# One channel tile of a depthwise convolution as diagonal products on TensorE, with three smaller edits around it

## The chip, the cores and the metric

The kernel runs on one core of one Trainium2 chip (trn2). The metric is device time in microseconds (us). TensorE is called PE in the profile (PEld is its weight load, PEclk its granted clock), VectorE is DVE, ScalarE is ACT, GpSimd is POOL, SyncE is SP. L970 is line 970 of the kernel's file.

## The reference, cut to what matters

A trunk of two layers works on 640 tokens of width 1024: 128 prompt tokens and 512 sample tokens. The change lies in layer 0, where one input projection feeds attention and a convolution module, and both share the output projection.

```python
h = x * (1 + scale) + shift                       # adaLN, vectors from silu(cond) @ w_ada
q, k, v, u = split(h @ w_in)                      # 512, 128, 128, 1024 columns
q, k = rmsnorm(q), rmsnorm(k)                     # per head of 64; rotary for sample tokens
att = softmax(q @ k.T / 8) @ v                    # 8 heads, 2 kv heads; sample sees 512 + 128 cached
a, gt = split(u, 2)
u = a * sigmoid(gt)                               # 512 channels
u = depthwise_conv(u, conv_w, width=31) + conv_b  # per channel, along the tokens of each request
u = silu(layernorm(u, conv_ln_g, conv_ln_b))      # over the 512 channels
x = layernorm(ALPHA * x + gate * (concat(att, u) @ w_out))
```

A squared-ReLU MLP, an mLSTM layer and a second MLP follow; the change leaves them alone.

## The kernel before, in words

Everything lives in SBUF as tiles of 128 partitions. A float32 operand of a large product is split into two fp32r parts, hi and lo, and every such product is three products on PE (`mm3`, L193 to L195). ScalarE makes the hi part of a weight piece (L166), GpSimd the lo part (L167).

The stage that the change touches runs in the profiled execution from about 62 to 325 us.

**Input projection, 62 to 186 us.** `GEMMS = "01k2qr3"` sets the order. A digit is a channel tile of the convolution: `glu(i)` makes two halves of the a and gate products (320 of the 640 tokens each), ScalarE takes tanh of the gate (`sg`, L977), VectorE multiplies into the padded array `up` (L981), and `conv(i)` (L950) follows. `k` is the key and value group, `q` and `r` two groups of query heads: five token tiles of products (128x256), evicted into the tile `acc`, then `chain`, which normalises per head on VectorE. `chain` calls `rsqrt_here` (L389), 15 short VectorE operations with three Newton steps; the conv norm calls it too.

**The convolution.** `up` has 128 channels on partitions and 655 output columns: 128 prompt tokens, 15 columns of padding, 512 sample tokens. A tap k is `cy += cw[k] * up[k:k+655]`. `CONV_DVE` says by channel tile which taps go to VectorE, as one operation each (L965; L956 for k = 0). Any other tap is an ACT product into a tile `tap` of two buffers (L970) and a GpSimd addition (L972). Tiles 0 and 1 have all 31 taps on VectorE, tile 2 every 4th, tile 3 every 8th. The conv has low priority (`CONV_BEHIND`): the framework's scheduler puts its taps behind other ready work, and so fixes the order of each engine's queue.

**Late adaLN vectors.** `background()` issues one k-step of a pending adaLN vector: four narrow PE products (128x32 weights, L293). After eight steps VectorE adds the bias (L297), and PE transposes the result (L305). Such steps stand between the tiles of the projection and between the units of attention. They use the one PSUM tile of `psc`.

**Attention, 186 to 325 us.** Twelve units (i, u): head pair i, u = -1 for the prompt rows, 0 and 1 for the sample rows. `weights_of` of the next unit makes scores (L1187), then `softmax`: VectorE maximum (L1152), ScalarE exp (L1154), VectorE reciprocal (L1155) and VectorE division (L1157). `values_of` transposes the weights on PE (L1219), copies them (L1222, L1224) and multiplies by v (L1226). Behind unit 8 (`NORM_AT`), the input rows are loaded again for the residual, and `conv_norm` runs in one piece: products with a matrix of ones for the mean (L1255, float32) and for the variance (L1269), `rsqrt_here`, diagonal products (L1280), and the swish.

Of the kernel before, what the change touches and what calls it, by code (L numbers as in the profile page):

```python
# [9 lines left out]
F32 = mybir.dt.float32  # L10
# [8 lines left out]
P = 128  # L19
# [39 lines left out]
LATE_DVE = 0  # L59
CONV_DVE = (range(31), range(31), range(0, 31, 4), range(0, 31, 8))  # L60
PT_ACT = (0,)
NORM_AT = 8
CN_DVE = (1, 1)
# [29 lines left out]
def trunk_kernel(ctx: ExitStack, tc: tile.TileContext, I, O):  # L93
# [297 lines left out]
    def rsqrt_here(out, var, n, scale):  # L391

        v, a = (smallp.tile([P, 20], F32, name=f"rh_{x}", bufs=1)[:, 0:n] for x in "va")
        g = out.bitcast(I32)
        nc.vector.tensor_scalar(out=v, in0=var, scalar1=scale, scalar2=EPS, op0=ALU.mult, op1=ALU.add)
        nc.vector.tensor_scalar(out=g, in0=v.bitcast(I32), scalar1=1, scalar2=None, op0=ALU.arith_shift_right)
        nc.vector.tensor_scalar(
            out=g, in0=g, scalar1=-1.0, scalar2=float(0x5F3759DF), op0=ALU.mult, op1=ALU.add)
        for _ in range(3):
            nc.vector.tensor_tensor(out=a, in0=out, in1=out, op=ALU.mult)  # L400
            nc.vector.tensor_tensor(out=a, in0=a, in1=v, op=ALU.mult)
            nc.vector.tensor_scalar(out=a, in0=a, scalar1=-0.5, scalar2=1.5, op0=ALU.mult, op1=ALU.add)
            nc.vector.tensor_tensor(out=out, in0=a, in1=out, op=ALU.mult)

    def rsqrt_one(r, var):
# [510 lines left out]
    with ExitStack() as m0s:  # L916
# [13 lines left out]
        if True:  # L930
            cvp = qcs.enter_context(tc.tile_pool(name="cvp", bufs=1, reuse_waits="tile"))
            cv2 = qcs.enter_context(tc.tile_pool(name="cv2", bufs=2, reuse_waits="tile"))
            qk = qcs.enter_context(tc.tile_pool(name="qk", bufs=1, reuse_waits="tile"))

            up = upp.tile([P, 4, UW], F32, name="up")
# [12 lines left out]
            S0 = PAD + SEQ + PAD  # L948

            def conv(i):  # L950

                y = cy[:, i, :]
                with tc.high_priority(offset=-CONV_BEHIND):
                    dve = CONV_DVE[i]
                    if 0 in dve:
                        nc.vector.tensor_scalar(  # L956
                            out=y, in0=up[:, i, 0:CW], scalar1=cw[:, i, 0:1], scalar2=cols[:, 64 + i:65 + i],
                            op0=ALU.mult, op1=ALU.add)
                    else:
                        nc.scalar.activation(  # L960
                            out=y, in_=up[:, i, 0:CW], func=AF.Identity, scale=cw[:, i, 0:1],
                            bias=cols[:, 64 + i:65 + i])
                    for k in range(1, CONV_K):
                        if k in dve:
                            nc.vector.scalar_tensor_tensor(  # L965
                                out=y, in0=up[:, i, k:k + CW], scalar=cw[:, i, k:k + 1], in1=y,
                                op0=ALU.mult, op1=ALU.add)
                        else:
                            tp = upp.tile([P, CW], F32, name="tap", bufs=2)
                            nc.scalar.activation(  # L970
                                out=tp, in_=up[:, i, k:k + CW], func=AF.Copy, scale=cw[:, i, k:k + 1])
                            nc.gpsimd.tensor_tensor(out=y, in0=y, in1=tp, op=ALU.add)  # L972
# [18 lines left out]
            def glu(i, steps=2):  # L991
                us = u_w[0] if i == 0 else u_units(i)
                for half in range(2):
                    ps = u_ps[half] if i == 0 else ps2()
                    pa, pg = ps[:, 0], ps[:, 1]
                    ks = range(4, 8) if i == 0 else range(KT)
                    fm_half(us[1], half, pg, ks)
                    fm_half(us[0], half, pa, ks)
                    background(steps)
                    gated(i, half, lambda: pa, pg)  # L1000
                conv(i)
# [51 lines left out]
            def chain(x, c0, n):  # L1053
# [10 lines left out]
                rr = smallp.tile([P, NT, n], F32, name=f"rr{n}", bufs=1)  # L1064
                rsqrt_here(
                    rr.rearrange("p t h -> p (t h)"), ss.rearrange("p t h -> p (t h)"), NT * n, 1.0 / HD)
# [21 lines left out]
            def kv_group():  # L1088
                ws = load_n256(w_in, ATT_W)
                put_k(ck, NT)  # L1090
                for t in range(NT):
# [3 lines left out]
                    nc.vector.tensor_copy(out=qkv[:, t, ATT_W:ATT_W + KV_W], in_=ps[:, 0:128])  # L1095
                    background(1)
                nc.sync.dma_start(out=O["new_cache_v"][0, 0], in_=vS[:, 0, :].rearrange("p (g d) -> p g d", d=HD))
                kn = chain(1, ATT_W, KVH)
# [3 lines left out]
            def q_group(grp, kn=None):  # L1102
                ws = load_n256(w_in, grp * 256)
                for t in range(NT):
                    ps = ps1()
                    tm_tile(ws, act, t, ps[:, 0:256])
                    nc.scalar.copy(out=qkv[:, t, grp * 256:(grp + 1) * 256], in_=ps[:, 0:256])
                    background(1)
                    if kn is not None:
                        put_k(kn[:, t], t)  # L1110
                chain(0, grp * 256, 4)

            kn = None
            for what in GEMMS:
                if what == "k":
# [3 lines left out]
                else:  # L1119
                    glu(int(what), 3)  # L1120
            drain()


# [22 lines left out]

        def softmax(ps, dst, multi):

# [7 lines left out]
            d2 = dst.rearrange("p a b -> p (a b)") if multi else dst  # L1156
            nc.vector.tensor_scalar(out=d2, in0=d2, scalar1=ri[:, 0:1], scalar2=None, op0=ALU.mult)  # L1157

# [5 lines left out]
        def weights_of(i, s):  # L1164
# [3 lines left out]
            if s < 0:  # L1168
# [6 lines left out]
                for h in range(2):  # L1175
                    softmax(sp[:, h, 0:P], pp[:, h, :], False)
                Ps[i, s] = pp
                return
            pts = [[], []]
            for t in (1 + 2 * s, 2 + 2 * s):  # L1180
                for h in range(2):
# [7 lines left out]
                    pt = att.tile([P, 2, HT], F32, name="ptok", bufs=PTOK)  # L1189
                    softmax(s2[:, :, 0:HT], pt, True)  # L1190
                    pts[h].append(pt.rearrange("p a b -> p (a b)"))
# [44 lines left out]
        def conv_norm():  # L1236
# [14 lines left out]
            for half in range(2):  # L1251
# [5 lines left out]
                for (c0, n, o) in segs(half):  # L1257
                    y = cy[:, :, c0:c0 + n]
                    nc.vector.tensor_tensor(out=y, in0=y, in1=wide(pm, o, n), op=ALU.subtract)
            sq = []  # L1260
            for i in range(4):
# [10 lines left out]
            rc = smallp.tile([P, NT], F32, name="rc", bufs=1)  # L1272
            rsqrt_here(rc, pv[:, 0:NT], NT, 1.0)
            for ts in ((0, 1, 2, 3), (4,)):
# [6 lines left out]
                for c0, n, o in ((0, P, 0), (PAD + P, 3 * P, P)) if len(ts) > 1 else ((PAD + 4 * P, P, 0),):  # L1281
                    y = cy[:, :, c0:c0 + n]
                    nc.vector.tensor_tensor(out=y, in0=y, in1=wide(pr, o, n), op=ALU.mult)

            for i in range(4):
# [6 lines left out]
                for c0, n, o in ((0, P, 0), (PAD + P, DEC, P)):  # L1292
                    hi, lo = (x[:, 4 + i, o:o + n] for x in act)
                    nc.scalar.copy(out=hi, in_=cy[:, i, c0:c0 + n])
                    CN_LO[i % 2].tensor_tensor(out=lo, in0=cy[:, i, c0:c0 + n], in1=f32(hi), op=ALU.subtract)

        ada_late = [(0, 5)] + [(1, v) for v in range(6)]
# [4 lines left out]
        for n, (i, u) in enumerate(units):  # L1302
# [6 lines left out]
            if n == NORM_AT:  # L1309
# [5 lines left out]
                cl = cls.enter_context(tc.tile_pool(name="cl", bufs=1, side="right", reuse_waits="tile"))  # L1315
                conv_norm()
        cls.close()
# [610 lines left out]
```

## Time and profile before

| | |
|---|---|
| median of three runs | 1735.19 us (1735.14 to 1742.12) |
| profiled execution | 1737.0 us, span 1735.2 us, mean granted clock 0.97 |
| PE busy | 1607.3 us, 93% of the span |
| DVE busy | 1098.1 us, 63% |
| ACT busy | 796.3 us, 46% |
| POOL busy | 1005.4 us, 58% |

The page gives shares over the whole program. The change touches only 62 to 325 us, so the views are asked for that stretch. A window's line gives each engine's busy time in it. A wait's line names the waiting instruction, then the one that it waited for. A group's line counts instructions of one source line and shape, with busy time and mean duration, and behind the last bar the idle time of that engine just before them.

### The profile page before, as it was taken

Reading aid. Unit: us, or ns where it says so; the run is one execution under the profiler, and the core shown is the slowest. Engines: PE = TensorE matmul, PEld = TensorE weight load, DVE = VectorE, ACT = ScalarE, POOL = GpSimd, SP = SyncE. Lnnn points to the kernel's source line nnn. Section 1 sums busy time; section 2 is a strip of 40 time slices with the busy share of each in tenths; the row PEclk is TensorE's granted clock in tenths of the full one; section 3 lists DMA queues with packets and bytes.
Section 4 is the critical chain, followed back from the end, with each engine's and each line's share of the span. In section 5 each row is a group of like instructions: output and inputs, shape, how many; then the busy total and the mean of one; then the engine's idle time right before and its main releaser. Section 6 shows DMA issues by size and latency. Waiting matters only on the chain. (4 is left out here: it accounts for less than half of the span.)

```text
span 1735.2 us, 27401 instructions
## 1 busy us (share of the span) xinstructions
PE 1607.3 (93%) x10155; PEld 1412.7 (81%) x10155; DVE 1098.1 (63%) x1924; ACT 796.3 (46%) x1560; POOL 1005.4 (58%) x760
## 2 busy tenths in 40 slices
PE   7988899998989999999788998997989999999996
PEld 4678555898879989987678998897979889989885
DVE  2899997669434444356875687778498354344367
ACT  2224666345444344343543555556265444344343
POOL 2246474247955546548654766756459756546565
PEclk8999999998999999999999999999999999999998
DMA  9852885323432213216223222235442323213241
GB/s 307 256 185 75 268 306 178 71 101 119 130 85 92 92 56 97 86 61 206 83 69 103 71 84 91 98 98 194 123 152 85 125 89 98 89 57 98 85 158 61
DMA packets 151309, 211.76 MB, mean 122 GB/s; under 512 B 11845, under 2 KB 92969, under 8 KB 151176
## 3 DMA queue, kind: packets, MB, share of 16 engines
q1 hardware_dynamic: 150944, 209.94, 37.4%
q8 instruction: 80, 1.31, 0.3%
q14 instruction: 53, 0.43, 0.1%
q10 hardware_dynamic: 232, 0.08, 0.0%
HBM read 186.74 MB, written 23.24 MB: 121 GB/s over the span
## 5 line engine op out<-in xcount | busy, mean ns | idle before, releaser
L167 POOL TENSOR_TENSOR wlo<-raw,whi 128x512 fp32r<-128x512 f32 x374 | 518.6, 1410 | 412.2 <-ACT whi L166 397.5
L166 ACT CAST whi<-raw 128x512 fp32r<-128x512 f32 x368 | 224.7, 620 | 429.2 <-PE ps L195 192.1
L193 PE MATMUL ps<-whi,h 128*128 128x512 f32 x640 | 254.5, 399 | 11.0 <-DVE pr L526 5.7
L194 PE MATMUL ps<-wlo,h 128*128 128x512 f32 x640 | 254.6, 398 | 0.3 <-POOL wlo L167 0.3
L195 PE MATMUL ps<-whi,h 128*128 128x512 f32 x640 | 253.6, 396 | 0.0
L193 PE MATMUL ps<-act_h,whi 128*128 128x320 f32 (+2 forms) x704 | 221.2, 316 | 8.5 <-ACT act_h L625 7.5
L194 PE MATMUL ps<-act_l,whi 128*128 128x320 f32 (+2 forms) x704 | 221.3, 315 | 5.5 <-DVE act_l L626 3.1
L195 PE MATMUL ps<-act_h,wlo 128*128 128x320 f32 (+2 forms) x704 | 220.9, 314 | 2.2 <-POOL wlo L167 2.2
L167 POOL TENSOR_TENSOR wlo<-s,whi 128x512 fp32r<-128x512 f32 x118 | 163.9, 1393 | 67.2 <-ACT whi L166 61.9
L758 DVE TENSOR_TENSOR acc<-acc,ps 128x512 f32<-128x512 f32 x120 | 81.8, 685 | 162.0 <-PE ps L195 162.0
L193 PEld LDWEIGHTS ps<-whi,h 128*128 128x128 f32 x640 | 121.3, 190 | 40.2 <-DVE pr L526 6.0
L193 PEld LDWEIGHTS ps<-act_h,whi 128*128 128x128 f32 x704 | 135.3, 192 | 13.2 <-ACT act_h L625 7.9
L195 PEld LDWEIGHTS ps<-whi,h 128*128 128x128 f32 x640 | 121.3, 190 | 29.2
L194 PEld LDWEIGHTS ps<-wlo,h 128*128 128x128 f32 x640 | 121.5, 190 | 28.1 <-POOL wlo L167 1.2
L194 PEld LDWEIGHTS ps<-act_l,whi 128*128 128x128 f32 x704 | 134.9, 192 | 8.9 <-DVE act_l L626 3.9
L195 PEld LDWEIGHTS ps<-act_h,wlo 128*128 128x128 f32 x704 | 134.9, 192 | 3.1 <-POOL wlo L167 3.1
L193 PE MATMUL ps<-whi,act_h 128*128 128x256 f32 x440 | 126.1, 290 | 0.3 <-DVE acc L1095 0.3
L194 PE MATMUL ps<-wlo,act_h 128*128 128x256 f32 x440 | 124.7, 287 | 0.0
L195 PE MATMUL ps<-whi,act_l 128*128 128x256 f32 x440 | 123.8, 287 | 0.0
L972 POOL TENSOR_TENSOR cy<-cy,tap 128x655 f32<-128x655 f32 x50 | 80.3, 1606 | 54.0 <-DVE cy L965 22.6
L193 PE MATMUL ps<-T_h,whi 128*128 128x320 f32 x336 | 103.7, 309 | 1.6 <-ACT pr L550 1.6
L166 ACT CAST whi<-s 128x512 fp32r<-128x512 f32 x120 | 73.2, 616 | 67.3 <-DVE s L501 54.9
(437 smaller groups left out, 4066.0 us busy)
## 6 DMA issues: line engine op xcount, KB each, us to landing
raw<-in_w_ff_dram SPq DMA_DIRECT2D x128, 512.0 KB
whi<-in_w_ada_dram SPq DMA_DIRECT2D x80, 256.0 KB
wlo<-in_w_ada_dram SPq DMA_DIRECT2D x80, 256.0 KB
raw<-in_w_in_m_dram SPq DMA_DIRECT2D x32, 512.0 KB
ada_w<-in_w_ada_dram SPq DMA_DIRECT2D x32, 256.0 KB
acc_d<-acc SPq DMA_DIRECT2D x15, 512.0 KB
raw<-in_w_in_a_dram SPq DMA_DIRECT2D x12, 512.0 KB
rx<-acc_d SPq DMA_DIRECT2D x20, 256.0 KB
```

Source lines behind the costliest of these rows:

```text
L166: nc.scalar.copy(out=hv, in_=src)
L167: (eng or nc.gpsimd).tensor_tensor(out=lv, in0=src, in1=f32(hv), op=ALU.subtract)
L193: nc.tensor.matmul(out=out, lhsT=lh, rhs=rh, start=start, stop=False)
L194: nc.tensor.matmul(out=out, lhsT=lh, rhs=rl, start=False, stop=False)
L195: nc.tensor.matmul(out=out, lhsT=ll, rhs=rh, start=False, stop=stop)
L758: nc.vector.tensor_tensor(out=x, in0=x, in1=ps, op=ALU.add)
L972: nc.gpsimd.tensor_tensor(out=y, in0=y, in1=tp, op=ALU.add)
```

## The change

Tile 0 of the convolution moves to PE. For each tap ScalarE makes a 128x128 diagonal matrix `dgt` (identity times that tap's 128 weights), and PE multiplies it by the shifted `up`: two float32 products, 512 sample columns and 128 prompt columns, summed over 31 taps in two PSUM banks (`psX`). `tap(2)` issues two taps at a time at 16 places of the projection, and ScalarE evicts the sum with the bias. For these banks the projection's other PSUM tiles are laid out anew after `glu(0)`. Of tile 3 now 8 taps instead of 4 are on VectorE. `rsqrt_root` replaces `rsqrt_here` in the three chains and the conv norm: one Sqrt on ScalarE and five VectorE operations. The softmax division of the first head of each pair goes to ScalarE. `conv_norm` becomes a generator of four steps, begun behind unit 7, with one step per unit.

```diff
-CONV_DVE = (range(31), range(31), range(0, 31, 4), range(0, 31, 8))
+CONV_DVE = (None, range(31), range(0, 31, 4), range(0, 31, 4))
-NORM_AT = 8
+NORM_AT = 7
...
+    def rsqrt_root(out, var, n, scale):
+        v, y, a = (smallp.tile([P, 20], F32, name=f"rq_{x}", bufs=1)[:, 0:n] for x in "vya")
+        nc.scalar.activation(out=y, in_=var, func=AF.Sqrt, bias=eps_t[:, 0:1], scale=scale)
+        nc.vector.tensor_scalar(out=v, in0=var, scalar1=scale, scalar2=EPS, op0=ALU.mult, op1=ALU.add)
+        nc.vector.reciprocal(out=y, in_=y)
+        nc.vector.scalar_tensor_tensor(out=a, in0=y, scalar=-0.5, in1=y, op0=ALU.mult, op1=ALU.mult)
+        nc.vector.tensor_tensor(out=a, in0=a, in1=v, op=ALU.mult)
+        nc.vector.scalar_tensor_tensor(out=out, in0=a, scalar=1.5, in1=y, op0=ALU.add, op1=ALU.mult)
...
+            dgp = dgs.enter_context(tc.tile_pool(name="dgp", bufs=4, reuse_waits="tile"))
...
+            def conv_pe(i):
+                ps = psX.tile([P, 2, 512], F32, name="psx")
+                nc.gpsimd.memset(cy[:, i, SEQ:SEQ + PAD], 0.0)
+                for k in range(CONV_K):
+                    if k:
+                        yield
+                    dg = dgp.tile([P, P], F32, name="dgt")
+                    nc.scalar.activation(out=dg, in_=ident, func=AF.Copy, scale=cw[:, i, k:k + 1])
+                    for j, (o, n) in enumerate(((S0 - PAD, DEC), (0, SEQ))):
+                        nc.tensor.matmul(
+                            out=ps[:, j, 0:n], lhsT=dg, rhs=up[:, i, o + k:o + k + n],
+                            start=(k == 0), stop=(k == CONV_K - 1))
+                for j, (o, n) in enumerate(((SEQ + PAD, DEC), (0, SEQ))):
+                    nc.scalar.activation(
+                        out=cy[:, i, o:o + n], in_=ps[:, j, 0:n], func=AF.Identity, bias=cols[:, 64 + i:65 + i])
+            def tap(n):
+                for _ in range(n):
+                    next(K.taps, None)
             def conv(i):
+                if CONV_DVE[i] is None:
+                    K.taps = conv_pe(i)
+                    return
...
             def glu(i, steps=2):
-                    ps = u_ps[half] if i == 0 else ps2()
-                    pa, pg = ps[:, 0], ps[:, 1]
+                    pa, pg = (u_ps[half][:, x] for x in range(2)) if i == 0 else (ps1() for _ in range(2))
...
                     background(steps)
+                    tap(2)
...
-                rsqrt_here(
+                rsqrt_root(
...
                     background(1)
+                    tap(2)
...
+                    if what == "0":
+                        psum_plan(0, 4)
...
+            tap(CONV_K)
             drain()
+            psum_plan(2, 2)
...
-            nc.vector.tensor_scalar(out=d2, in0=d2, scalar1=ri[:, 0:1], scalar2=None, op0=ALU.mult)
+            if on_act:
+                nc.scalar.activation(out=d2, in_=d2, func=AF.Copy, scale=ri[:, 0:1])
+            else:
+                nc.vector.tensor_scalar(out=d2, in0=d2, scalar1=ri[:, 0:1], scalar2=None, op0=ALU.mult)
...
-                    softmax(sp[:, h, 0:P], pp[:, h, :], False)
+                    softmax(sp[:, h, 0:P], pp[:, h, :], False, h == 0)
...
-                    softmax(s2[:, :, 0:HT], pt, True)
+                    softmax(s2[:, :, 0:HT], pt, True, h == 0)
...
-            rsqrt_here(rc, pv[:, 0:NT], NT, 1.0)
+            rsqrt_root(rc, pv[:, 0:NT], NT, 1.0)
...
-                conv_norm()
+                norm = conv_norm()
+            if n >= NORM_AT:
+                next(norm, None)
```

In `conv_norm`, a `yield` stands behind the mean, behind the variance's products and scaling, and behind the second of the four channel tiles of the swish.

The scheduler sets the order that results. PE, in the key and value group, between two token tiles (L293 is a step of a late adaLN vector). Before:

```order
L195 MATMUL ps_942<-whi,act_l 128x256
L293 MATMUL psc<-whi,stat 32x256 x2
L293 MATMUL psc<-wlo,stat 32x256 x2
L193 MATMUL ps_977<-whi,act_h 128x256
L194 MATMUL ps_977<-wlo,act_h 128x256
```

After:

```order
L195 MATMUL ps_989<-whi,act_l 128x256
L293 MATMUL psc<-whi,stat 32x256 x2
L293 MATMUL psc<-wlo,stat 32x256 x2
L972 MATMUL psx<-up,dgt 128x512
L972 MATMUL psx<-up,dgt 128x128
L972 MATMUL psx<-up,dgt 128x512
L972 MATMUL psx<-up,dgt 128x128
L193 MATMUL ps_1032<-whi,act_h 128x256
L194 MATMUL ps_1032<-wlo,act_h 128x256
```

Two taps, four products, have come in; there are 16 such places, all before attention. Over the whole attention stretch the L293 steps stand in 39 groups where there were 49, since some steps have moved ahead of it.

VectorE, at the key chain (`ss` is the sum of squares, `rr` the inverse root). Before:

```order
L1063 TENSOR_REDUCE ss_1141<-qk_s_1139 128x10
L965 SCALAR_TENSOR_TENSOR cy<-up,cw,cy 128x655 x2
L395 TENSOR_SCALAR rh_v<-ss_1141 128x10
L965 SCALAR_TENSOR_TENSOR cy<-up,cw,cy 128x655 x2
L396 TENSOR_SCALAR rr_1143<-rh_v 128x10
L965 SCALAR_TENSOR_TENSOR cy<-up,cw,cy 128x655 x2
L397 TENSOR_SCALAR rr_1143<-rr_1143 128x10
```

After:

```order
L1001 SCALAR_TENSOR_TENSOR cy<-up,cw,cy 128x655 x2
L1099 TENSOR_REDUCE ss_1185<-qk_s_1183 128x10
L409 TENSOR_SCALAR rq_v<-ss_1185 128x10
L410 RECIPROCAL rq_y<-rq_y 128x10
L411 SCALAR_TENSOR_TENSOR rq_a<-rq_y 128x10
L412 TENSOR_TENSOR rq_a<-rq_a,rq_v 128x10
L413 SCALAR_TENSOR_TENSOR rr_1187<-rq_a,rq_y 128x10
L1103 TENSOR_TENSOR acc<-acc,rr_1187 128x5x128
```

The taps between the steps of the chain are gone, and the chain's reciprocal L410 reads what ScalarE's Sqrt writes.

ScalarE, at the chain of the second query group. Before:

```order
L1061 ACTIVATE qk_s_1805<-acc 128x1280
L1136 CAST qs<-acc 128x2x64
L970 ACTIVATE tap<-up,cw 128x655 x2
L1050 CAST kTA<-po 128x2x128
L970 ACTIVATE tap<-up,cw 128x655
L977 ACTIVATE sg<-ps_1855 128x320
```

After:

```order
L1097 ACTIVATE qk_s_1905<-acc 128x1280
L1006 ACTIVATE tap<-up,cw 128x655 x2
L1013 ACT_TABLE_LOAD
L1013 ACTIVATE sg<-ps_1948 128x320
L408 ACT_TABLE_LOAD
L408 ACTIVATE rq_y<-ss_1907,eps_t 128x20
L1013 ACT_TABLE_LOAD
L1013 ACTIVATE sg<-ps_2002 128x320
```

Each change between tanh and Sqrt brings a table load. The whole program has 14 of them where it had 7.

## Rows read from the trace of the kernel before

**Rows 1.** Part 1 of the page: busy us, share of span, instructions of each engine.

```profile
PE 1607.3 (93%) x10155; PEld 1412.7 (81%) x10155; DVE 1098.1 (63%) x1924; ACT 796.3 (46%) x1560; POOL 1005.4 (58%) x760
```

**Rows 2.** Windows of the stage; columns are named in the first line.

```profile
core 0: us, PE busy (x) PEld busy (x) DVE busy (x) ACT busy (x) POOL busy (x), PEclk, DMA share, GB/s
62.00:123.00 61.00, 60.69 (x488) 51.69 (x487) 57.95 (x73) 13.35 (x26) 23.36 (x16) 0.97 0.63 209
123.00:164.00 41.00, 31.33 (x237) 30.17 (x236) 40.52 (x70) 16.70 (x37) 24.50 (x17) 0.92 0.24 73
...
186.00:206.00 20.00, 16.73 (x125) 8.74 (x124) 17.43 (x34) 14.78 (x35) 9.69 (x8) 0.85 0.82 283
206.00:286.00 80.00, 75.50 (x622) 39.87 (x622) 70.18 (x145) 55.55 (x115) 55.09 (x38) 1.00 0.83 288
...
62.00:186.00 124.00, 110.07 (x876) 98.00 (x876) 118.96 (x182) 40.19 (x81) 57.79 (x39) 0.95 0.51 166
186.00:325.00 139.00, 130.54 (x1002) 75.30 (x1002) 118.95 (x247) 87.48 (x181) 67.32 (x48) 0.97 0.62 213
```

**Rows 3.** PE's waits, 62 to 186 us: what waits, for what, us in total, times, longest.

```profile
PE psc L305 <- DVE ada_m L297: 6.6, 1, 6.6
PE ps L1187 <- DVE up L981: 2.4, 1, 2.4
PE po L1046 <- DVE kTB L1051: 2.1, 1, 2.1
```

**Rows 4.** PE's waits, 186 to 325 us.

```profile
PE psc L293 <- DVE ada_m L297: 2.9, 1, 2.9
PE ps L1140 <- DVE qs L1137: 2.7, 4, 1.1
...
PE psc L305 <- DVE ada_m L297: 0.9, 1, 0.9
```

**Rows 5.** Tile cy: ns min/median/max, first and last start us, forms.

```profile
L972 POOL TENSOR_TENSOR cy<-cy,tap x50: 1339/1582/2670, 131.2 to 270.0; 128x655 f32<-128x655 f32 x50
...
L1255 PE MATMUL psc<-cy,ones x24: 274/326/433, 289.3 to 296.9; 128*128 128x128 f32 x8, 128*128 128x192 f32 x8, 128*128 128x320 f32 x8
```

**Rows 6.** Timeline of PE, 289 to 298 us: start us, us, instruction.

```profile
289.31 2.36 PE L1255 MATMUL psc<-cy,ones 128*128 128x128 f32 x16
...
295.01 2.31 PE L1255 MATMUL psc<-cy,ones 128*128 128x320 f32 x8
```

**Rows 7.** Timeline of PEld, 81 to 83 us; idle before in brackets.

```profile
81.28 0.14 PEld L293 LDWEIGHTS psc<-whi,stat 128*32 128x32 f32 x4
81.84 0.19 PEld L194 LDWEIGHTS ps<-wlo,act_h 128*128 128x128 f32 x1 [0.41 <-issue]
```

**Rows 8.** Groups by line and shape, VectorE, 62 to 325 us: busy, mean ns.

```profile
L965 DVE SCALAR_TENSOR_TENSOR cy<-up,cw,cy 128x655 f32<-128x655 f32 x70 | 74.5, 1085 | 0.5
...
L1157 DVE TENSOR_SCALAR ptok<-ptok,ri 128x640 f32<-128x640 f32 x32 | 28.7, 896 | 0.5
...
L403 DVE TENSOR_TENSOR rr<-rh_a,rr 128x20 f32<-128x20 f32 x6 | 2.1, 356 | 0.1
```

**Rows 9.** The same for ScalarE; behind | idle before, by releaser.

```profile
L970 ACT ACTIVATE tap<-up,cw 128x655 f32<-128x655 f32 x50 | 41.9, 841 | 36.1 <-POOL cy L972 28.6 <-DVE up L981 7.5
...
L1154 ACT ACTIVATE ptok<-ps,nm 128x640 f32<-128x640 f32 x32 | 25.5, 797 | 15.5 <-DVE nm L1152 6.9 <-PE ps L1219 5.9 <-DVE rh_a L401 2.0
...
L1136 ACT CAST qs<-acc 128x128 fp32r<-128x128 f32 x20 | 6.1, 304 | 2.3 <-DVE acc L1068 2.2
```

**Rows 10.** Timeline of ACT, 898 to 904 us.

```profile
899.22 1.28 ACT L1571 ACT_TABLE_LOAD   x1
900.51 0.74 ACT L1571 ACTIVATE g_ab<-g_ab 64x640 f32<-64x640 f32 x1
```

**Rows 11.** ScalarE's longest wait, 62 to 325 us: us in total, times, longest.

```profile
ACT tap L970 <- POOL cy L972: 28.6, 18, 4.9
```

More of the change, by code (lines that the diff above doesn't have):

```diff
@@ L933, in trunk_kernel @@
             qk = qcs.enter_context(tc.tile_pool(name="qk", bufs=1, reuse_waits="tile"))
+            dgs = ExitStack()
+            dgp = dgs.enter_context(tc.tile_pool(name="dgp", bufs=4, reuse_waits="tile"))
             up = upp.tile([P, 4, UW], F32, name="up")
@@ L1108, in q_group @@
                     background(1)
+                    tap(2)
                     if kn is not None:
@@ L1113, in trunk_kernel @@
             kn = None
+            K.taps = iter(())
             for what in GEMMS:
@@ L1120, in trunk_kernel @@
                     glu(int(what), 3)
+                    if what == "0":
+                        psum_plan(0, 4)
+                        psP = K.psum.enter_context(tc.tile_pool(name="psP1", bufs=1, space=PSUM, reuse_waits="tile"))
+                        psX = K.psum.enter_context(tc.tile_pool(name="psX", bufs=1, space=PSUM, reuse_waits="tile"))
+            tap(CONV_K)
+            dgs.close()
             drain()
+            psum_plan(2, 2)
+            psP = K.psum.enter_context(tc.tile_pool(name="psP2", bufs=1, space=PSUM, reuse_waits="tile"))
         att = m0s.enter_context(tc.tile_pool(name="att", bufs=2, reuse_waits="tile"))
@@ L1145, in prep, with softmax @@
             qTs[i] = qT
-        def softmax(ps, dst, multi):
+        def softmax(ps, dst, multi, on_act):
             nm = smallp.tile([P, 1], F32, name="nm")
@@ L1259, in conv_norm @@
                     nc.vector.tensor_tensor(out=y, in0=y, in1=wide(pm, o, n), op=ALU.subtract)
+            yield
             sq = []
@@ L1283, in conv_norm @@
                     nc.vector.tensor_tensor(out=y, in0=y, in1=wide(pr, o, n), op=ALU.mult)
+            yield
             for i in range(4):
@@ L1295, in conv_norm @@
                     CN_LO[i % 2].tensor_tensor(out=lo, in0=cy[:, i, c0:c0 + n], in1=f32(hi), op=ALU.subtract)
+                if i == 1:
+                    yield
         ada_late = [(0, 5)] + [(1, v) for v in range(6)]
@@ L1315, in trunk_kernel @@
                 cl = cls.enter_context(tc.tile_pool(name="cl", bufs=1, side="right", reuse_waits="tile"))
-                conv_norm()
+                norm = conv_norm()
+            if n >= NORM_AT:
+                next(norm, None)
+        for _ in norm:
+            pass
         cls.close()
```

## The prediction

> **What bounds the kernel now.** Begin with the page's busy shares [rows 1]: PE has 93% of the span, VectorE 63%. That says only which engine to suspect; the change touches 263 of 1735 us, so the next view is the windows of that stretch [rows 2]. Two things are to be seen there. In the projection, 62 to 186 us, VectorE is busy for 119.0 of 124 us, and PE, full at first (60.7 of 61), falls to 31.3 of 41 us between 123 and 164. In attention, 186 to 325 us, PE has 130.5 of 139 us and VectorE 119.0. So VectorE fills the first half and PE nearly fills both. The third view, PE's waits, tells how much of PE's idle time is VectorE's doing. In the projection 13.9 us are idle (124 less 110.07), and 11.1 of them are three waits for VectorE: 6.6 for a bias addition L297, 2.4 for `up` L981, 2.1 for a key copy L1051 [rows 3]. These are short operations that stood behind convolution taps. In attention 8.5 us are idle, 6.5 of them for VectorE [rows 4].
>
> The granted clock is the last thing to read from the windows. It is 0.92 in 123 to 164 and 0.85 in 186 to 206, while it is 1.00 from 206 to 286 [rows 2]. Between the levels of 1.2 and 2.4 GHz, 0.92 means that 16% of 41 us, 6.6 us, ran at the lower one, and 0.85 that 30% of 20 us, 6.0 us, did. Both stretches are those in which PE was least busy.
>
> **The work that PE gets.** Its price must come from another float32 product, since the trace has no `dgt` yet. The mean of the conv norm, L1255, is one: twelve products in the code, 24 rows in the trace, so each runs as two. A row of 128 columns lasts 274 ns, one of 320 lasts 433 [rows 5]: 159 ns for 192 columns, 0.828 ns a column. Rows overlap, so the step between them counts, not the duration: eight rows of 320 take 2.31 us in all [rows 6], hence (2.31 - 0.433) / 7 = 0.268 us a step, which is the same 0.83 to 0.84 ns a column. A row of 512 columns then steps by 0.427 us and one of 128 by 0.109. A tap is two of each: 1.07 us. 31 taps are **+33.2 us** on PE, all in the projection.
>
> Each of the 16 places could also cost a break, as the one after four narrow L293 products, where the weight load sits 0.41 us idle [rows 7]. In the order the diagonal products mostly stand behind such an L293 step, which has its break already; so I count none, and keep 16 x 0.41 = 6.6 us for the upper bound (39.8).
>
> **What VectorE loses.** A tap lasts 1.085 us [rows 8]; 74 taps become 47 (31 of tile 0 go, 4 of tile 3 come): -29.3. Sixteen of the 32 large divisions at 0.896 us leave: -14.3. Short operations of the four inverse roots go from 60 to 20, at 0.356 us [rows 8]: -14.2. That is 58 of 238 us. In the projection VectorE will have much slack, and the three waits of 11.1 us and attention's 6.5 us should go: **-11.1** and **-6.5**. As the reciprocal now waits for ScalarE's Sqrt, conv taps and evictions queue behind it on VectorE, and PE waits for the evictions; but this is four waits of about a table load, some 5 us against 58 of slack, so nothing.
>
> With the waits gone, the clock should stay up: in the two stretches PE was busy for some 4.0 of the 6.6 us and 5.5 of the 6.0, and at half speed half of that is lost: **-4.8**. And ten fewer L293 groups in attention spare ten breaks of 0.41: **-4.1**. (Steps that moved into the projection lie beside other steps or the diagonal products.)
>
> **What ScalarE gains.** The 31 `dgt` are like a 128x128 cast of 0.304 us [rows 9]: 9.4. Sixteen divisions at the 0.797 of an exp of that shape: 12.8, and four small ones. Four taps fewer at 0.841: -3.4. Seven table loads of 1.28 us [rows 10]: 9.0. Together about 29 on the 127.7 of 263 us it has now [rows 2], so it is not full, and the divisions and diagonals are hidden in its 135 idle us. What isn't hidden is one load between a chain's gate products and PE's next need of `up`: **+1.3** (bounds: none, or all seven, 9.0). In rows 10 the next ACTIVATE follows a load at 0.01 us (899.22 + 1.28 = 900.50, against 900.51), so I count the load alone. The Trainium skill, "ScalarE: Activation LUTs", What ACT_TABLE_LOAD costs, adds a drain of about 1380 ns to about 1283 ns of load. The trace agrees with the load (1.28 us) and doesn't show the drain behind it; by the page's figure the one load would cost an estimated 2.7 instead of 1.3.
>
> **Counted at nothing.** The conv norm does the same PE products in four pieces. It starts about a unit earlier: 139 us over twelve units is some 11 us. GpSimd's last conv addition starts at 270.0, the first mean product at 289.3 [rows 5], so 19 us of cover become 8, and GpSimd has four additions of 1.58 less. If that cover went, PE would wait for `cy`. The four single PSUM banks hold two halves of `glu` as two double ones did. On SP's queue the loads of adaLN weights keep their places; those of x pass output weights by a few places, and are needed only after attention.
>
> **The sum.** 33.2 - 11.1 - 6.5 - 4.8 - 4.1 + 1.3 = **+8.0 us** on the profiled execution's 1737.0, so 1745.0. The median of the three runs is 1.8 us below the profiled execution, so I say **1743**. What the change buys on VectorE is worth only what PE waited for it; what it costs stands on PE. The case's own range is 1736 to 1751: below, more of PE's other idle time closes; above, the 6.6 us of breaks.
>
> **Rivals.**
> *PE closes every gap* (chance 0.14). All 22.4 us of idle go (13.9 + 8.5), and the clock is full throughout: at 0.95 over 124 us and 0.97 over 139 [rows 2], 12.4 + 8.3 us were at the lower level, and with PE's share of some 0.8 busy half of that is 8.3. Then 33.2 - 22.4 - 8.3 - 4.1 = -1.6: 1733.6, no change. For it: nearly all waits shown are VectorE's. Against it: some idle was for weights, and new waits arise.
>
> *ScalarE's queue becomes the limit* (0.21). It runs in order, and a tap waits there for GpSimd's addition, 28.6 us in 18 waits, the longest 4.9 [rows 11]. Behind such a tap now stand diagonals, Sqrts and divisions that PE or VectorE need. If all seven loads (7.7 more) and one longest wait lie on PE's path, that is 8.0 + 7.7 + 4.9 = +20.6: 1755.8. It decides once PE's waits for ScalarE pass some 9 us. For it: all new helpers' work lands on this one engine. Against it: it is busy under half of the time.
>
> *Faster: attention was VectorE's, not PE's* (0.09). PE's rows overlap, and its weight loads fill only 75.3 of 139 us there [rows 2]. VectorE loses 14.3 of large divisions, and about 10 more there (small divisions, the norm's root, five taps that come earlier): 119 becomes 95. If attention's length follows VectorE, at the present 119 of 139 it would be 111 us, at the 119 of 124 of the projection 99. The projection gains 33.2 - 11.1 - 2.0 + 1.3 = 21.4, so the sum is -7 to -19; middle -13, thus **1722**. It decides where PE's rows in attention fall under some 115 us. Against it: PE is shown idle for 8.5 us only, and the 622 rows of 206 to 286 step by 0.12 us on average. The Trainium skill, "Perfetto Trace Analysis", Identifying the Most-Contended Engine, speaks for this rival: since matmuls are pipelined, PE's busy share is a poor measure of headroom, and the busy share of weight loads a better one; by that rule the stretch would have room, and the rows' idle time says little.
>
> **How the numbers follow.** The forecast case has 0.56, the rivals 0.14, 0.21 and 0.09. About 0.5%, 8.7 us, is what a measurement of this kernel can tell from no change: the bounds are 1726.5 and 1743.9. My case straddles the upper one: 0.32 of it within, 0.24 above. With the gap-closing case in the middle, ScalarE's above and the last below: faster 0.09, same 0.46, slower 0.45. The range of 1730 to 1757 holds the first three cases and leaves out the fast one and the worst of ScalarE's.
>
> **What would show it right or wrong.** Right: 62 PE rows of 512 and 62 of 128 columns at L972, with steps near 0.43 and 0.11; the wait at L305 gone; the projection some 18 us longer and attention some 10 to 13 shorter; a granted clock near 1 in both; VectorE near 180 us in the stage. Wrong: PE waits for ScalarE's lines L970, L1006 or L1013 of over 9 us; diagonal products that step by more; an attention under 120 us; or PE idle again for VectorE, behind the reciprocal.

## The result and the profile after

The changed kernel takes 1750.92 us (median of five, 1747.39 to 1753.86), the kernel before 1736.98 us in the five runs beside it. The ratio is 1.0066, with a 95% interval of 1.0052 to 1.0081: 11.5 us slower, between 9.0 and 14.1. (The two medians stand 13.9 us apart, inside that interval.) The forecast was 8 us slower, 1743, with a range of 1730 to 1757.

The profiled execution took 1753.56 us. Part 1 of its page, beside [rows 1]:

```profile
PE 1635.0 (93%) x10279; PEld 1428.4 (82%) x10279; DVE 1033.5 (59%) x1837; ACT 827.1 (47%) x1620; POOL 985.6 (56%) x757
```

PE has 124 more rows, two for each of 62 products, and 28 us more to do; VectorE 65 us less. The windows of the stage, with the columns of [rows 2]; the border between projection and attention is drawn at 200 us here:

```profile
123.00:164.00 41.00, 41.00 (x285) 32.62 (x283) 12.33 (x24) 26.08 (x55) 28.91 (x23) 1.00 0.21 66
...
286.00:336.00 50.00, 44.62 (x288) 29.38 (x286) 37.07 (x77) 30.78 (x58) 4.02 (x4) 0.88 0.22 77
62.00:200.00 138.00, 138.00 (x1002) 113.09 (x1000) 73.67 (x125) 64.01 (x124) 60.24 (x46) 0.99 0.44 141
200.00:336.00 136.00, 127.29 (x1000) 75.26 (x998) 101.99 (x230) 97.11 (x204) 48.81 (x36) 0.96 0.64 226
```

In the projection PE has no gap: 138.0 of 138 us, at a clock of 0.99; the list of its waits there is empty, where [rows 3] had 11.1 us. VectorE has fallen to 73.7. But the last 50 us of attention show a clock of 0.88 and 5.4 us of idle PE. PE's waits in attention, which answer to [rows 4], say for what:

```profile
PE po L1276 <- DVE pT L1274: 3.5, 4, 1.4
PE ps L1187 <- DVE qs L1184: 2.3, 3, 1.0
...
PE psc L305 <- DVE ada_m L297: 0.4, 1, 0.4
PE ps L1237 <- ACT ptok L1201: 0.4, 1, 0.4
```

The waits for the bias addition (L297) are all but gone: 0.4 us where [rows 4] had 3.8. Those for `qs` have stayed, 2.3 us where there were 2.7. A new one heads the list, for copies of attention weights (`pT`). The timeline of VectorE in the last attention unit shows why:

```profile
324.71 0.69 DVE L1274 COPY pT<-ps 128x512 f32<-128x512 f32 x1 [0.77 <-PE ps L1269]
325.32 1.14 DVE L1341 TENSOR_SCALAR cy<-cy,hgb 128x655 f32<-128x655 f32 x2
326.38 0.83 DVE L1343 SCALAR_TENSOR_TENSOR cy<-csq,cy 128x655 f32<-128x655 f32 x1
...
328.41 0.68 DVE L1274 COPY pT<-ps 128x512 f32<-128x512 f32 x1
...
330.29 0.89 DVE L1347 TENSOR_TENSOR act_l<-cy,act_h 128x128 fp32r<-128x128 f32 x2
331.09 0.68 DVE L1274 COPY pT<-ps 128x512 f32<-128x512 f32 x1
```

Most of the swish of the conv norm (L1341, L1343, and the lo parts of its result, L1347) stands ahead of the last four copies and between them, though PE needs the copies at once. Before, all of it came behind the last copy:

```profile
323.30 0.69 DVE L1224 COPY pT<-ps 128x512 f32<-128x512 f32 x1 [0.48 <-PE ps L1219]
323.91 1.14 DVE L1289 TENSOR_SCALAR cy<-cy,hgb 128x655 f32<-128x655 f32 x2
```

PE's timeline of the changed kernel beside it:

```profile
329.15 0.65 PE L1276 MATMUL po<-pT,vS 128*64 128x256 f32 x4 [0.97 <-DVE pT L1274]
...
331.83 1.12 PE L1276 MATMUL po<-pT,vS 128*64 128x256 f32 x4 [1.44 <-DVE pT L1274]
```

PE waits 0.97 and 1.44 us for the first two of these copies. Behind the waits the same four products take 1.12 us instead of 0.65, at a granted clock of 0.52 from 331 to 336 us.

Where did the 11.5 us arise? Four marks in each trace tell: the first write of `up`, the first prompt scores, the prompt values of the last head pair, the last value product. Two of the marks are the first start of the scores' line and the last start of the values' line, in the trace before and then in the one after:

```profile
L1173 PE MATMUL ps<-kTA,qT x8: 275/284/327, 181.7 to 279.4; 128*128 128x128 f32 x8
...
L1226 PE MATMUL po<-pT,vS x160: 379/404/431, 213.8 to 324.3; 128*64 128x256 f32 x160
```

```profile
L1223 PE MATMUL ps<-kTA,qT x8: 273/286/328, 202.4 to 285.5; 128*128 128x128 f32 x8
...
L1276 PE MATMUL po<-pT,vS x160: 379/430/689, 224.9 to 335.9; 128*64 128x256 f32 x160
```

The first `up` starts at 61.1 and 61.2, the last pair's prompt values at 307.7 and 314.1. The windows between the marks, before and then after:

```profile
61.10:181.70 120.60, 108.75 (x870) 97.14 (x870) 115.59 (x177) 40.56 (x82) 56.80 (x38) 0.96 0.50 162
181.70:307.70 126.00, 115.85 (x909) 66.01 (x906) 108.23 (x214) 81.40 (x170) 68.30 (x48) 0.97 0.71 243
307.70:324.30 16.60, 15.91 (x101) 10.27 (x102) 14.29 (x40) 5.38 (x10) 0.00 (x0) 0.90 0.00 1
```

```profile
61.20:202.40 141.20, 140.20 (x1015) 113.76 (x1015) 75.64 (x131) 66.33 (x129) 62.17 (x48) 0.99 0.45 144
202.40:314.10 111.70, 108.74 (x896) 65.80 (x894) 80.57 (x188) 83.14 (x176) 46.88 (x35) 0.98 0.76 266
314.10:335.90 21.80, 16.82 (x96) 8.94 (x94) 20.16 (x40) 11.66 (x23) 0.00 (x0) 0.81 0.04 12
```

So the projection grew from 120.6 to 141.2 us (+20.6), attention up to the last pair shrank from 126.0 to 111.7 (-14.3), and the last pair grew from 16.6 to 21.8 (+5.2): together +11.5. In the last pair PE's idle time grew from 0.7 to 5.0 us, its busy time from 15.9 to 16.8, at a clock of 0.81 instead of 0.90. That the stage's 11.5 is the ratio's 11.5 too is partly chance: the spans of these two executions differ by 16.4, and the other 4.9 us arise behind the stage.

### The profile page after: what moved, and what is told of

Same layout as the page of the kernel before. It is cut to its first block, busy times and chain, and to the rows that moved or that the text cites. A ratio compares the mean times of both kernels' runs of the same rounds, so it can differ in the third digit from the quotient of the medians.

```text
span 1751.6 us, 27636 instructions
## 1 busy us (share of the span) xinstructions
PE 1635.0 (93%) x10279; PEld 1428.4 (82%) x10279; DVE 1033.5 (59%) x1837; ACT 827.1 (47%) x1620; POOL 985.6 (56%) x757
## 4 chain that ended last, share of the span: by engine, by line
PE 65%; DVE 16%; DMA 9%; POOL 4%; ACT 4%; issue 3%; SPq 0%; DVEq 0%; POOLq 0%; ACTq 0%
PE ps L193 17%; PE ps L194 17%; PE ps L195 17%; DMA raw<-in_w_in_m_dram 2%; POOL wlo L167 2%; PE psc L293 2%; PE psx L972 2%; DMA ada_w<-in_w_ada_dram 2%; DMA raw<-in_w_ff_dram 1%; DVE act_l L636 1%; PE po L1276 1%; PE ps L1269 1%; DVE wt L1743 1%; PE ps L1237 1%; ACT whi L166 1%
## 5 line engine op out<-in xcount | busy, mean ns | idle before, releaser
L167 POOL TENSOR_TENSOR wlo<-raw,whi 128x512 fp32r<-128x512 f32 x374 | 510.6, 1386 | 387.2 <-ACT whi L166 369.3
L193 PEld LDWEIGHTS ps<-act_h,whi 128*128 128x128 f32 x704 | 135.8, 193 | 11.5 <-ACT act_h L635 7.9
L193 PE MATMUL ps<-whi,act_h 128*128 128x256 f32 x440 | 126.0, 289 | 0.0
L509 DVE TENSOR_TENSOR s<-raw 128x512 f32<-128x512 f32 x40 | 47.4, 1184 | 97.9 <-DMA raw<-in_w_ff_dram 68.9
```

Of the source, the lines that this page charges most:

```text
L167: (eng or nc.gpsimd).tensor_tensor(out=lv, in0=src, in1=f32(hv), op=ALU.subtract)
L193: nc.tensor.matmul(out=out, lhsT=lh, rhs=rh, start=start, stop=False)
L509: tt(out=s3, in0=m11, in1=m21, op=ALU.subtract)
```

## Experiments

Every kernel is compared with the kernel before on the same chip. Each has one trace, so the spread of the stretches below is not known, and a difference of 1 or 2 us in them says little; the times before range from 1732 to 1747 us over all runs. The table gives the ratio, and from each trace three stretches of the stage, in us: first `up` to first prompt values (8 to 18 us behind the first prompt scores); from there to the prompt values of the last pair; from there to the last value product.

| kernel | ratio (95%) | to values | to last pair | last pair | stage |
|---|---|---|---|---|---|
| before | 1 | 139.1 | 107.5 | 16.6 | 263.2 |
| the change | 1.0066 (1.0052 to 1.0081) | 150.8 | 102.1 | 21.8 | 274.7 |
| swish_behind | 1.0039 (1.0025 to 1.0054) | 151.2 | 103.4 | 17.5 | 272.1 |
| tile0_dve | 1.0047 (1.0029 to 1.0066) | 134.4 | 106.3 | 22.0 | 262.7 |
| short_taps | 0.9981 (0.9967 to 0.9996) | 135.2 | 109.9 | 16.4 | 261.5 |
| pe_only | 1.0214 (1.0198 to 1.0230) | 154.3 | 107.3 | 17.5 | 279.1 |
| others_behind | 1.0007 (0.9989 to 1.0025) | 133.2 | 107.9 | 17.7 | 258.8 |
| half_pe | 1.0089 (1.0062 to 1.0115) | 136.4 | 112.7 | 17.6 | 266.7 |
| here | 1.0077 (1.0061 to 1.0092) | 152.4 | 109.4 | 15.0 | 276.8 |
| noact | 1.0152 (1.0129 to 1.0175) | 150.4 | 107.8 | 19.8 | 278.0 |
| roots_and_division | 1.0030 (1.0013 to 1.0048) | 135.3 | 104.3 | 26.0 | 265.6 |
| others_behind_t3 | 1.0027 (1.0008 to 1.0046) | 133.9 | 106.0 | 22.1 | 262.0 |

**1. The swish behind the copies (swish_behind).**

```diff
+            while not K.done:
+                yield
+            hg2 = cl.tile([P, 8], F32, name="hg2")
+            nc.vector.scalar_tensor_tensor(out=hg2, in0=K.pT[:, 0:8], scalar=0.0, in1=hgb, op0=ALU.mult, op1=ALU.add)
...
-                    out=y, in0=y, scalar1=hgb[:, i:i + 1], scalar2=hgb[:, 4 + i:5 + i], op0=ALU.mult, op1=ALU.add)
+                    out=y, in0=y, scalar1=hg2[:, i:i + 1], scalar2=hg2[:, 4 + i:5 + i], op0=ALU.mult, op1=ALU.add)
```

> The changed kernel with one thing moved: VectorE's part of the conv norm's swish reads its constants from a tile that is made from the last copied attention weights, so that it can't stand ahead of the last copies. Theory (the sum held, and the 5 us that it misses are lost in the last attention unit, where the swish stands ahead of four copies that PE waits for): PE's waits for the copies fall from 3.5 to under 0.5 us, the last head pair takes 17 us instead of 22, the kernel is 4 to 6 us faster than the change, so 6 to 8 us over before. Rival (the last unit is slow because the divisions and table loads on ScalarE come late; the copies are only what is seen): within 2 us of the change, 11 to 14 us over before.

1.0039 is 6.8 us over before, 4.7 less than the change; the last pair takes 17.5 us, 4.3 less. Of PE's waits in attention the copies keep 1.0 and 0.8 us, more than the 0.5 that was expected:

```profile
PE po L1278 <- DVE pT L1276: 1.0, 2, 0.8
PE ps L1270 <- DVE pT L1276: 0.8, 1, 0.8
```

The theory holds, but for what is left of the waits: the swish's place costs 4 to 5 us. The rival, that the copies are only what is seen, would have left the last pair slow, which it isn't; by the time alone, with these intervals, it would just be out. (The stage as a whole is only 2.6 us shorter; attention ahead of the last pair is 1.3 longer than the change's.)

**2. Tile 0 back on VectorE (tile0_dve).**

```diff
-CONV_DVE = (None, range(31), range(0, 31, 4), range(0, 31, 4))
+CONV_DVE = (range(31), range(31), range(0, 31, 4), range(0, 31, 4))
```

> The changed kernel with tile 0 of the convolution back on VectorE; the other three edits stay. Theory (PE's products are the price, and VectorE's relief buys only what PE waited): without the products PE has no more work than before, the projection's three waits come back in part, attention's gain stays: 1722 to 1736, about 9 us below before. Rival (ScalarE's queue of Sqrts, divisions and table loads is what costs): not faster than before, 0 to 6 us over it.

The stage is 12.0 us shorter than the change's, so that is what the products cost there net of what they bring. Up to the last pair it is 5.9 us ahead of before; the last pair gives 5.4 back. The time is another matter: 8.2 us over before, where 9 below were expected, and the stage explains none of it. Most of it arises in the first MLP, where PE has a wait of 7.1 us for VectorE that the trace before doesn't have. VectorE's and GpSimd's timelines show on what:

```profile
PE ps L193 <- DVE c L533: 7.1, 1, 7.1
```

```profile
437.28 12.51 DVE L509 TENSOR_TENSOR s<-raw 128x512 f32<-128x512 f32 x1 [3.93 <-DMA raw<-in_w_ff_dram]
449.71 0.81 DVE L732 TENSOR_TENSOR h<-c,h 128x640 fp32r<-128x640 f32 x1
```

```profile
436.47 2.94 POOL L636 TENSOR_TENSOR act_l<-h,act_h 128x1280 fp32r<-128x1280 f32 x1
439.32 5.04 POOL L167 TENSOR_TENSOR wlo<-raw,whi 128x512 fp32r<-128x512 f32 x4
444.25 1.33 POOL L455 TENSOR_TENSOR rx<-rx,lnt 128x512 f32<-128x512 f32 x1
445.46 2.56 POOL L167 TENSOR_TENSOR wlo<-raw,whi 128x512 fp32r<-128x512 f32 x2
447.91 1.33 POOL L455 TENSOR_TENSOR rx<-rx,lnt 128x512 f32<-128x512 f32 x1
```

One subtraction lasted 12.5 us while GpSimd ran without a gap, and ended 0.55 us behind GpSimd's row; the same line took at most 2.1 us in the trace before. No code there was changed, but VectorE's order is another: the operation L732 that PE's next work needs now stands behind the subtraction, where it stood ahead of it. The rival, that ScalarE's new work is what costs, foresaw a time of 0 to 6 us over before; PE's wait is for VectorE instead. So from here on the stage and the time are read apart.

**3. Short taps (short_taps).**

```diff
                     for j, (o, n) in enumerate(((S0 - PAD, DEC), (0, SEQ))):
+                        n = n if k in (0, CONV_K - 1) else n // 8
```

> The changed kernel, with 28 of the 31 diagonal taps multiplied over 64 and 16 columns instead of 512 and 128; the rest of the convolution of tile 0 is left out. Diagonals, waits and places are the same. Theory (PE is without a gap in the projection, so each us of product is a us of the kernel): a tap falls from 1.09 us to some 0.3, 28 times 0.8 is 22 us, about 1728, 9 to 12 us below before. Rival (the tap's pace is set by ScalarE's diagonals, or VectorE limits again as soon as PE is shorter): less than half of that, no faster than 1740.

Two shortened taps take 0.92 us (87.25 to 88.17) instead of 2.18 at this place. Added up over the 16 places of each trace, the diagonal products take 14.5 us instead of 32.9, so they save 18.4 us, not 22:

```profile
87.25 1.07 PE L973 MATMUL psx<-up,dgt 128*128 128x64 f32 x8
88.17 0.36 PE L193 MATMUL ps<-whi,act_h 128*128 128x256 f32 x1
```

The stretch to the first values is 15.6 us shorter than the change's: most of it, so there PE is the limit, as the theory has it. The time lies between theory and rival: 3.3 us below before, where the theory had 9 to 12. 3.6 of the missing us are the mis-sized tap. And attention up to the last pair takes 7.8 us longer than the change's, of which the last pair gives 5.4 back. In that stretch of attention PE idles 5.5 us where it idled 2.5 in the change's, and its granted clock is 0.95 instead of 0.98. All of VectorE's relief is in this kernel, so relief alone does not make attention short.

**4. PE alone (pe_only).** Tile 3, roots, division and norm as before; tile 0 on PE.

> The kernel before with tile 0 on PE alone: tile 3, the inverse roots, the division and the norm in one piece stay as before. Theory: 33.9 us of products, less 11.1 us of waits and 2 of clock in the projection, and little in attention: 17 to 21 us over before, 1754 to 1758. The other edits would then be worth some 8 us to the change. Rival (VectorE's taps held attention up too, and the other edits are worth nothing): 11 to 14 us over before, as the change.

The stage is 15.9 us longer, a little under the 17 to 21; the time is 37 us longer, and there the forecast missed. Behind the stage VectorE waits for the adaLN gate's load, and PE for VectorE:

```profile
DVE s L461 <- DMA h<-gate_d: 27.4, 4, 8.9
```

```profile
PE ps L193 <- DVE s L461: 17.2, 4, 7.2
```

In the trace before VectorE waits 1.4 us for that load, in the change's 9.6. Why it lands late was not tried. In the stage the other edits are worth 4.4 us to the change (279.1 against 274.7), and 8.7 up to the last pair (261.6 against 252.9), where some 8 were expected.

**5 and 6. The others with the swish behind (others_behind), and 14 taps on PE (half_pe).** The first joins the edits of 1 and 2.

> Tile 0 back on VectorE, the other three edits, and VectorE's part of the swish tied behind the last copies of attention weights. Theory (the other edits gain 6 us up to the last head pair, the swish ahead of the copies gave 5 back, the rest of the 8 us of the run with tile 0 on VectorE arose behind the stage): attention ends 5 to 8 us earlier than before, the last pair takes 17 us; the time is 4 to 8 us below before if nothing new stalls behind the stage, so 1730 to 1738. Rival (the other edits cost by themselves, through ScalarE): within 3 us of the run with tile 0 on VectorE.

The stage is 4.4 us shorter than before, where 5 to 8 were expected, and the last pair takes 17.7: the theory's mechanism, at a little less than its size. The time is that of before, so the 4 to 8 us were missed. The first MLP takes the gain back: PE waits there 10.9 us, 5.7 in the trace before, for an operation that stands on VectorE behind one that waits for its weights:

```profile
PE ps L193 <- DVE pr L536: 10.9, 1, 10.9
```

The second run moves taps 0 to 13 of tile 0, one at each place:

```diff
-                for k in range(CONV_K):
+                for k in range(PE_TAPS):
...
+                        nc.vector.tensor_tensor(
+                            out=cy[:, i, o:o + n], in0=cy[:, i, o:o + n], in1=ps[:, j, 0:n], op=ALU.add)
```

> As the run before it, but 14 of tile 0's 31 taps on PE, one at each place, added to VectorE's sum at the end. Theory (PE takes products free as long as it would have waited, then each costs 1.09 us; 31 taps cost 34 us and 22 were absorbed): 14 taps, 15 us, are absorbed, the attention's end within 3 us of the run without products. Rival (each tap costs in proportion, 12 us over 31): 5 us later than that run.

Up to the first values 15 us of products cost 3.2 us, so most was absorbed, as the theory had it. But attention up to the last pair is 4.8 us longer, and the stage 7.9: worse than the rival's 5. The windows of that stretch, of run 5 and then of run 6, show what makes it longer:

```profile
195.30:303.20 107.90, 101.36 (x830) 60.82 (x828) 77.96 (x175) 80.06 (x164) 50.51 (x37) 0.98 0.70 240
```

```profile
198.10:310.80 112.70, 107.01 (x822) 65.60 (x818) 77.94 (x175) 76.65 (x158) 43.82 (x32) 0.92 0.66 228
```

PE does not idle longer (5.7 us against 6.5). It is busy for 5.7 us more with no more rows, at a clock of 0.92 instead of 0.98. Between the levels of 1.2 and 2.4 GHz that is 18 us at the lower one instead of 4, and half of the difference, an estimate of 7 us, is more than the whole loss. Why the clock fell was not tried. The time is 14 us over run 5's, 7.9 of them in the stage; behind it PE waits 9.7 us for VectorE at the gate's line (L462).

**7. The roots as before (here), and 8. all divisions on VectorE (noact).**

```diff
-                rsqrt_root(
+                rsqrt_here(
```

> The changed kernel with the inverse roots as before, in 15 short operations of VectorE without Sqrt; tile 0 on PE, division and norm in steps as changed. The order then has the swish behind the last copies. Theory (VectorE has slack; the roots' gain is nothing once the taps are gone, and what remains of them are table loads and the forward swish): 4 to 7 us faster than the change, 5 to 8 over before at attention's end. Rival (the short chains were what PE waited for at the start of attention): slower than the change.

The last pair takes 15.0 us, as the order promised, but attention ahead of it is 7.3 us longer than the change's, and nothing is won: 1.0077 against 1.0066 is no difference. My theory falls. For the rival speaks that PE's wait for `qs` is 5.3 us where the change has 2.3; but this covers 3.0 of the 7.3 us, and the time is not clearly longer.

```diff
-                    softmax(s2[:, :, 0:HT], pt, True, h == 0)
+                    softmax(s2[:, :, 0:HT], pt, True, False)
```

> The changed kernel with all softmax divisions on VectorE. Theory (PE sets attention's pace once the taps are gone, VectorE has 34 of 136 us idle there): the head pairs keep their pace within 2 us, the swish stands among the last copies and costs less, so 0 to 4 us faster than the change. Rival (the division on ScalarE is where attention's gain came from): attention 6 to 9 us longer, slower than the change.

Attention is 5.7 us longer up to the last pair, which then takes 2.0 less; the stage is 3.3 longer, the time 15 us longer than the change's. (The trace is of the fastest of the five executions, 1758.9 us where the median is 1766.0; where the rest of the 15 us arises it can't show.) The rival was nearer, but by run 3 a stretch can be as long with the division shared, so that the division is where the gain came from is not shown.

**9 and 10. Roots and division alone.** Once on the kernel before (norm in one piece), once as run 5 with tile 3 as before.

> The kernel before with only the inverse roots through Sqrt and the shared division: all of tile 0 and tile 3 as before, the norm in one piece behind unit 8. The order has all but one operation of the swish behind the last copies. Theory (VectorE's relief of some 28 us, with nothing put on PE, shortens attention by what roots and division are worth): attention ends 5 to 9 us earlier; of that, the first MLP's wait for its weights, 5.7 us before, takes a part back: 2 to 6 us faster than before. Rival (VectorE's relief in the projection finds no use without fewer taps; Sqrt's table loads cost the rest): within 2 us of before.

> As the run with tile 0 on VectorE and the swish tied behind the copies, with tile 3's taps shared as before (every 8th on VectorE), so roots, division and the norm in steps. Theory: attention ends 4 to 8 us earlier than before, the last pair takes 17 us, and the first MLP's weights take a part back: 1 to 5 us faster than before. Rival (tile 3's four taps on VectorE were needed so that GpSimd ends in time for the early norm): slower than the run with them.

The stage should have ended 5 to 9 and 4 to 8 us earlier; it ended 2.4 later and 1.2 earlier, and the times are 5.2 and 4.7 us over before. Both are 7 us ahead of before at the start of the last pair (239.6 and 239.9 against 246.6), and both lose it in that pair: 26.0 and 22.1 us against 16.6. In the first, the swish stands ahead of the last four copies, other than the expectation had read the order; the softmax division of the last unit stands behind the swish too, and PE waits for it:

```profile
PE ps L1269 <- DVE ptok L1207: 4.7, 1, 4.7
```

In the second the swish is behind the copies, and why the pair takes 22.1 us is open: PE idles 3.9 us in it, at a clock of 0.85. Its first MLP has run 2's long subtraction again, 12.8 us, and a wait of PE of 7.3 us behind it. The lead never reaches the time; in both the expected gain did not come. No version that does the whole convolution beat the kernel before.

## Why the prediction was right

**The products: right.** The two taps at 89.98 us end PE's turn at 92.16, 1.09 us a tap against the 1.07 that was worked out. The seven places behind an L293 step take 2.18 to 2.19 us a pair, the eight other pairs 2.08; with the single tap at the last place it is 32.9 us in all, against 33.2.

```profile
89.98 2.43 PE L972 MATMUL psx<-up,dgt 128*128 128x512 f32 x8
92.16 0.37 PE L193 MATMUL ps<-whi,act_h 128*128 128x256 f32 x1
```

**The breaks: right to count none.** Only seven of the 16 places stand behind an L293 step, not most. There the 0.41 us stand before the diagonal's first load, and behind the last one the next load follows at once. At the other nine the first diagonal row comes 0.12 us behind the row before, as ordinary rows do. The loads at the place shown:

```profile
89.98 0.30 PEld L972 LDWEIGHTS psx<-up,dgt 128*128 128x128 f32 x2 [0.41 <-issue]
...
92.14 0.19 PEld L193 LDWEIGHTS ps<-whi,act_h 128*128 128x128 f32 x1
```

**What PE waited for in the projection: right in sum.** 33.2 - 11.1 - 2.0 + 1.3 was 21.4; the projection grew by 20.6, and its clock rose from 0.95 to 0.99. Run 3 shows that PE sets its pace. The 1.3 us for a table load appear nowhere, since PE has no wait there, and more idle time closed than the listed waits: by the marks 11.9 us became 1.0. Part of the closeness is the border's: the forecast drew it at 186 us, and the wait of 2.4 us for `up` lies between 181.7 and 186, so by the marks the forecast was 23.8 for the projection and -15.8 for attention.

**Attention's gain: right in size up to the last pair, its reasons in part.** 6.5 + 2.8 + 4.1 was 13.4; up to the last pair it is 14.3. By the marks PE's idle time there fell from 10.2 to 3.0 us, its busy time from 115.9 to 108.7. But of the 6.5 us of waits the 2.7 for `qs` stayed, and the clock of attention did not rise: 0.97 before, 0.96 now. That the clock was low where PE was least busy was too simple a reading: from 164 to 186 us PE was busy for 18.05 of 22 us at 0.98, from 186 to 206 for 16.73 of 20 at 0.85. The 4.1 us of breaks have no run of their own. Attention as a whole, with its last pair, is 9.1 us shorter, just outside the 10 to 13 that were named.

I took VectorE's relief as one sum of 58 us with slack to spare (VectorE is at 175.7 us in the stage, against the 180 forecast). Where the gain lies shows that no single part of it can be given the credit. Most of it, 8.9 of the 14.3 us, lies between the first prompt scores and the first prompt values, before and then after:

```profile
181.70:200.20 18.50, 13.02 (x95) 6.65 (x92) 16.71 (x31) 9.75 (x22) 9.20 (x7) 0.82 0.79 261
```

```profile
202.40:212.00 9.60, 9.13 (x76) 4.86 (x74) 7.45 (x17) 8.61 (x22) 7.36 (x6) 1.00 1.04 387
```

In this short stretch before lay the waits of 2.9 us for L297 and 2.4 for `up`, and all ten variants take 8 to 10 us for it, with the taps off VectorE, with the roots and the division, or with both. The other 5.4 us lie behind it. There runs 2, 4, 7 and 8, which lack the relief from the taps, the roots or the division, are 4 to 7 us longer than the change. That would mean that each part was needed, but run 3 has every part and is 7.8 us longer, so this is not shown; what kept PE's idle time at 2.5 us there in the changed kernel stays open.

**ScalarE: right.** It gained 33 us in the stage (161.1 against 127.7; 31 in the whole program) where 29 were forecast: a diagonal takes 0.40 us instead of 0.30, a division 0.83 instead of 0.80. PE waits for it 0.4 us, so the second rival is out.

```profile
L1205 ACT ACTIVATE ptok<-ptok,ri 128x640 f32<-128x640 f32 x16 | 13.3, 832 | 2.8 <-DVE ri L1202 2.8
...
L970 ACT ACTIVATE dgt<-ident,cw 128x128 f32<-128x128 f32 x27 | 10.8, 401 | 21.6 <-PE psx L972 21.6
```

The loads between tanh and Sqrt can be seen one by one:

```profile
190.23 1.28 ACT L408 ACT_TABLE_LOAD   x1
191.52 0.31 ACT L408 ACTIVATE rq_y<-ss,eps_t 128x20 f32<-128x20 f32 x1
191.85 1.28 ACT L1013 ACT_TABLE_LOAD   x1
193.15 0.44 ACT L1013 ACTIVATE sg<-ps 128x320 f32<-128x320 f32 x1
```

A load takes 1.28 us. The Trainium skill, "ScalarE: Activation LUTs", What ACT_TABLE_LOAD costs, adds a drain of some 1380 ns to each. The trace agrees with the load and shows no drain: from one function's end to the load it is 0.02 us, from the load's end to the next function 0.01 to 0.02.

**The conv norm "counted at nothing": wrong, and the term that the sum lacked.** I asked only whether the norm could start early, and compared the last conv addition with the first mean product. What it cost lies at its end. In the new order most of the swish stands in the last unit, ahead of four copies that PE waited for; with the lower clock behind the waits that is 5.2 us. Run 1 takes 4.3 of them back in the last pair, 4.7 in the time. 20.6 - 14.3 + 5.2 is 11.5; the forecast without that term was 8.0. It was luck that the projection and attention came out 0.8 and 0.9 us better than forecast: this hid 1.7 of the 5.2.

**The other rivals.** PE closed every gap, but only in the projection. Attention was not VectorE's alone: PE's rows still fill 127.3 of its 136 us, where the third rival asked for under 115.

## What to carry to other kernels

Work that moves from a full engine to a nearly full one is priced by the waits that it removes there; here 33 us of products bought back some 21 in the stage. Where a scheduler orders the queues, a relief can move later operations forward too: look at the end of the stage for work that now stands ahead of what the bound engine needs, and at the unchanged stages behind it, where the time of these variants moved by up to 21 us though no code was changed (run 4: 37 us in time, 16 in the stage). Compare by marks in the trace as well as by total time.

## What the hardware showed

A subtraction on VectorE that took 0.7 to 2.1 us in the trace before lasted 12.5 us, from 437.28 to 449.79, while GpSimd's operations followed one another without a gap until 449.24 (run 2). In run 10 the same line lasted 12.8 us, from 434.34 to 447.11, beside a like row of GpSimd that ended at 446.55. The Trainium skill, "SBUF — State Buffer", SBUF: two separate sides, says that the two share a port pair, held for a whole instruction while the other blocks. The trace before agrees with one instruction: there the subtraction began beside an operation of GpSimd that ended at 437.62 and ended itself at 438.17, though GpSimd's row went on without a gap to 445.54. In runs 2 and 10 it was held through nine operations, and ended 0.55 us behind the last of them. So a row without gaps does not by itself decide; what does stays open, and no run tried to break the row.

A float32 product runs as two rows. At 320 columns each steps by 0.84 ns a column (0.268 us, [rows 6]). Two taps are 2560 columns of rows and take 2.08 us, 0.81 ns a column, or 2.18 behind an L293 step, 0.85.
